# A decoder layer in float32: the dense products of 512 columns written as two of 256 columns

## The chip, the cores and the metric

The kernel runs on one core of a Trainium2 chip. The metric is the device time of one execution in microseconds. A core has a matrix engine (PE, TensorE), a vector engine (DVE, VectorE), a scalar engine (ACT, ScalarE), POOL (GpSimd) and SP (SyncE), which issues most DMAs. A product on PE has a stationary operand (the weights, loaded by an instruction of its own that the profile shows on a row PEld) and a moving operand, whose columns stream through; its result goes to PSUM, in banks of 512 float32 columns.

## The reference

One layer of a decoder over 512 tokens of width 1024: a norm, one combined projection, four token mixers (sliding-window attention, a convolution module, forgetting attention, block-sparse attention), each projected and gated, an output projection, and a feed-forward part with a causal convolution of width 3.

```python
h = rmsnorm(x, ln1_g)
z = h @ w_in
...
proj = jnp.einsum('bsnc,ncd->bsnd', branches, w_br)
merged = jnp.einsum('bsnd,bsnd->bsd', gates, proj)
x = x + merged @ w_out
h2 = rmsnorm(x, ln2_g)
u = causal_depthwise_conv(h2 @ w_up, ffn_conv_w, ffn_conv_b)
g_ff, v_ff = jnp.split(u, 2, axis=-1)
return x + (jax.nn.silu(g_ff) * v_ff) @ w_down
```

A last norm follows. All tensors are float32.

## The kernel before

Activations lie transposed, 128 channels by 512 tokens, so a tile of the result is 128 output channels by all 512 tokens, which is one PSUM bank. To keep precision with the one-pass type float32r, each operand is split into a high part (a rounded copy, by ACT, line 179) and a low part (the rest, by DVE, line 180), and a product is made of three: high by high, low by high, high by low. The names are whi and wlo for weights, hh and hl for the normed activations (both 8 tiles of 128 channels deep), and y with two planes for the outputs of the mixers, 4 tiles deep.

The work is a list of units, written out in order. A dense unit is made by `t_mm` (lines 232 to 247): it takes a PSUM tile `dps` of three that rotate, and for each of nk tiles k multiplies (wh, mh), (wl, mh), (wh, ml) into it, 3 x nk products of 512 columns with the weights as the stationary operand. It serves the combined projection except for the v columns, the gates, the up-projection (nk = 8, moving hh and hl) and the branch projections (nk = 4, moving y). Not made by it are the v units (line 294, 24 products of 256 columns, the first four of them 264), the attention products (lines 451, 452, 506, 565, 566, 624), the output projection (lines 967 and 1009) and the down-projection (line 1118). In line 506 a head multiplies v, as the stationary operand, with PTh and then with PTl, in widths of 512, 384, 256 and 128; line 624 does the same for the sliding window in widths of 256 and 128 with va as the stationary operand (odd heads keep both parts in one tile PT). In line 1118 the activations ah and al are stationary and the weights move; its last tile of 128 tokens uses two banks of 256 columns each (`wps`), and its last 8 of 22 weight tiles lie resident in wdh and wdl, which take the buffers of hh and hl (same tags).

The main loop (from line 1393 on) takes the units in turn: pieces of attention heads go on PE ahead of the unit's own products, then the previous unit's result is taken out of PSUM, then the splits of the next weights and the loads are issued. PE runs its instructions in the order written; semaphores tell it when weights are split and when a PSUM bank is free. `DVE P` of line 472 is the scaling of the softmax, `DVE sm` of line 584 a sum in the sliding window's softmax.

Of the kernel before, what the change touches and what calls it, by code (L numbers as in the profile page):

```python
# [53 lines left out]
def hybrid_layer_kernel(ctx: ExitStack, tc: tile.TileContext, x, ln1_g, w_in, b_gate, b_fgate, sinks,  # L54
# [3 lines left out]
    PE, ACT, DVE, SP = nc.tensor, nc.scalar, nc.vector, nc.sync  # L58
# [20 lines left out]
    def dense_ps():  # L79
        return PD.tile([128, 512], F32, name="dps", tag="dps", bufs=3)  # L80
# [66 lines left out]
    class Raw:  # L147


        def __init__(self, parts, nk, w):  # L150
            self.parts, self.nk, self.w = parts, nk, w
            self.idx, self.left = len(raws), 0
            raws.append(self)
# [70 lines left out]
        return [Half(raw, slice(k, k + 4), slice(0, n)) for k in (0, 4)]  # L224


    class Unit:
        def __init__(self, hs, mm, ev, adv=True):
            self.hs, self.mm, self.ev, self.adv = hs, mm, ev, adv
# [2 lines left out]
    def t_mm(hf, c0, mh, ml, nk):  # L232

        def go(mid=None, at_k=0):
            ps = dense_ps()
            h = hf[0]
            n = 0
            for k in range(nk):
                if mid and k == at_k:
                    mid()  # L240
                wh, wl = h.hi[:, k, c0:c0 + 128], h.lo[:, k, c0:c0 + 128]
                for a, b in ((wh, mh(k)), (wl, mh(k)), (wh, ml(k))):
                    PE.matmul(ps, lhsT=a, rhs=b, start=n == 0, stop=n == 3 * nk - 1)  # L243
                    n += 1
            return ps
        return go
# [959 lines left out]
    for half, end in ((0, NF), (1, KRES)):  # L1206
        for k0 in range(0, end, 4):
            nk = min(4, end - k0)
# [292 lines left out]
```

## Time and profile before

| | us |
|---|---|
| median of 3 runs (lowest to highest) | 1014.49 (1014.19 to 1014.76) |
| the profiled execution's own time | 1014.47 |
| its span, first to last instruction | 1012.7 |
| PE busy | 1001.2 |
| PEld busy (weight loads) | 824.6 |
| DVE busy | 667.0 |
| ACT busy | 448.3 |

Products on PE overlap in its pipeline: a product's duration in the profile is the time from its start to its modelled end, and the next one starts well before that. What a product takes from the time is the distance from its start to the next start. It is read from the timeline (start times) or from the chain of work that ended last, where a run of products of one kind stands as one piece with a start, a length and a count.

### The profile page before, as it was taken

How to read it: one execution, taken by the hardware profiler on the slowest of the kernel's cores; microseconds unless marked ns; L12 is line 12 of the kernel's file. 1: busy time of each engine (PE TensorE's matmuls, PEld its weight loads, DVE VectorE, ACT ScalarE, POOL GpSimd, SP SyncE). 2: the span in 40 equal slices, each digit the busy share in tenths (PEclk: the TensorE clock that was granted, in tenths of full speed). 3: DMA queues.
4: the chain of work that ended last, by engine and by line, in shares of the span. 5: the costliest groups of instructions: out<-in, count | busy, mean ns of one | idle time of the engine just before them, and what ended most of it. 6: DMA issues, size and time to landing. Idle time of an engine off the chain costs nothing.

```text
span 1012.7 us, 12462 instructions
## 1 busy us (share of the span) xinstructions
PE 1001.2 (99%) x4840; PEld 824.6 (81%) x4840; DVE 667.0 (66%) x1188; ACT 448.3 (44%) x782; POOL 23.2 (2%) x49
## 2 busy tenths in 40 slices
PE   8999999999999999999999999999999999999997
PEld 6878887989888888888888888888888888888886
DVE  6557777777878688896665445677776677733404
ACT  6435455455455545556423233443444444432202
POOL 1300000000000000000000000000000000000000
PEclk9999999999999999999999999999999999999999
DMA  7335522132233133232135430232223223334102
GB/s 254 102 113 185 164 85 85 42 105 81 66 108 121 42 83 100 64 99 93 42 125 205 149 125 1 84 125 84 83 94 114 83 84 99 130 124 146 63 1 84
DMA packets 101099, 102.18 MB, mean 101 GB/s; under 512 B 3377, under 2 KB 88544, under 8 KB 101040
## 3 DMA queue, kind: packets, MB, share of 16 engines
q1 hardware_dynamic: 99264, 99.31, 31.0%
q0 software_dynamic: 1200, 1.03, 0.4%
q10 hardware_dynamic: 576, 1.05, 0.3%
q8 instruction: 38, 0.62, 0.2%
q14 instruction: 21, 0.17, 0.1%
HBM read 99.10 MB, written 7.51 MB: 105 GB/s over the span
## 4 chain that ended last, share of the span: by engine, by line
PE 92%; DVE 4%; ACT 2%; issue 1%; DMA 1%; SPq 0%; DVEq 0%; ACTq 0%
PE dps L243 63%; PE wps L1118 8%; PE dps L1118 5%; PE dps L294 4%; PE dps L1009 2%; PE wps L967 2%; PE tps L479 2%; PE yps L506 1%; PE sps L452 1%; PE sps L451 1%; ACT P L434 1%; PE yps L624 1%; DMA raw<-in_w_in_dram 1%; DVE stE L383 1%; DVE P L472 1%
## 5 line engine op out<-in xcount | busy, mean ns | idle before, releaser
L243 PE MATMUL dps<-hh,whi 128*128 128x512 f32 x848 | 336.0, 396 | 0.0
L243 PE MATMUL dps<-hh,wlo 128*128 128x512 f32 x848 | 335.3, 395 | 0.0
L243 PE MATMUL dps<-hl,whi 128*128 128x512 f32 x848 | 335.1, 395 | 0.0
L180 DVE TENSOR_TENSOR wlo<-raw,whi 128x1024 fp32r<-128x1024 f32 (+1 forms) x152 | 185.5, 1222 | 95.4 <-ACT whi L179 95.2
L179 ACT ACTIVATE whi<-raw 128x1024 fp32r<-128x1024 f32 (+1 forms) x152 | 159.6, 1055 | 98.0 <-PE wps L1118 37.9
L243 PEld LDWEIGHTS dps<-hh,wlo 128*128 128x128 f32 x848 | 159.8, 188 | 37.1
L243 PEld LDWEIGHTS dps<-hl,whi 128*128 128x128 f32 x848 | 159.1, 188 | 37.1
L243 PEld LDWEIGHTS dps<-hh,whi 128*128 128x128 f32 x848 | 159.2, 188 | 36.8 <-ACT v L304 0.2
L434 ACT ACTIVATE P<-P,nm 128x128 f32<-128x128 f32 (+2 forms) x96 | 50.9, 531 | 76.4 <-DVE nm L432 75.8
L243 PE MATMUL dps<-y,whi 128*128 128x512 f32 x256 | 83.6, 397 | 0.0
L707 DVE SCALAR_TENSOR_TENSOR co<-hc,pcB,co 128x489 f32<-128x489 f32 (+25 forms) x120 | 82.5, 729 | 0.4
L1082 DVE SCALAR_TENSOR_TENSOR uy<-u,pcC,uy 128x511 f32<-128x511 f32 x88 | 65.8, 747 | 1.5
L243 PEld LDWEIGHTS dps<-y,whi 128*128 128x128 f32 x256 | 48.3, 189 | 10.9
L1074 DVE TENSOR_TENSOR u<-dps,rb 128x512 f32<-128x512 f32 x44 | 30.2, 687 | 37.3 <-PE dps L243 34.6
L243 PE MATMUL dps<-y,wlo 128*128 128x512 f32 x128 | 50.7, 396 | 0.0
L492 ACT ACTIVATE PTh<-tps 128x512 fp32r<-128x512 f32 (+1 forms) x48 | 24.4, 525 | 43.6 <-PE tps L479 43.3
L1118 PE MATMUL wps<-whi,al 128*128 128x512 f32 (+1 forms) x116 | 42.6, 367 | 0.0
L1118 PE MATMUL wps<-whi,ah 128*128 128x512 f32 (+1 forms) x116 | 42.6, 367 | 0.0
L1118 PE MATMUL wps<-wlo,ah 128*128 128x512 f32 (+1 forms) x116 | 42.5, 366 | 0.0
L1096 ACT ACTIVATE ah<-uy 128x512 fp32r<-128x512 f32 x22 | 13.9, 632 | 60.4 <-DVE uy L1095 60.4
L536 ACT ACTIVATE ytmp<-yps 64x512 f32<-64x512 f32 x24 | 14.3, 595 | 48.6 <-PE yps L506 25.0
L1088 ACT ACTIVATE uy<-uy 128x512 f32<-128x512 f32 x22 | 13.9, 632 | 43.7 <-DVE uy L1082 43.7
(250 smaller groups left out, 1291.9 us busy)
## 6 DMA issues: line engine op xcount, KB each, us to landing
raw<-in_w_up_dram SPq DMA_DIRECT2D x22, 1024.0 KB, 5.1
raw<-in_w_in_dram SPq DMA_DIRECT2D x40, 512.0 KB, 3.9
raw<-in_w_in_dram SPq DMA_DIRECT2D x14, 1024.0 KB, 5.1
raw<-in_w_down_dram SPq DMA_DIRECT2D x10, 1024.0 KB, 5.0
raw<-in_w_br_dram SPq DMA_DIRECT2D x16, 512.0 KB, 3.4
Gw<-Gd SPq DMA_DIRECT2D x8, 640.0 KB, 6.9
x<-in_x_dram SPq DMA_DIRECT2D x8, 512.0 KB, 8.4
raw<-in_w_out_dram SPq DMA_DIRECT2D x4, 1024.0 KB, 4.9
```

The source lines that it names most:

```text
L179: yield ACT.activation(self.hi, src, AF.Copy)
L180: yield DVE.tensor_tensor(self.lo, src, f(self.hi), op=OP.subtract)
L243: PE.matmul(ps, lhsT=a, rhs=b, start=n == 0, stop=n == 3 * nk - 1)
L294: PE.matmul(ps[:, :n], lhsT=l, rhs=r[:, k % 4, :], start=not done, stop=len(done) == 3 * KD - 1)
L434: ACT.activation(P[:, sl], P[:, sl], AF.Exp, bias=nm[:, i:i + 1], scale=-1.0, accum_out=sm[:, i:i + 1])
L479: PE.transpose(ps[:, c:c + 128], o["P"][:, PO[qb] + kb * 128:PO[qb] + kb * 128 + 128], ident)
L492: ACT.activation(o["PT"][0][:, sl], ps[:, :c], AF.Copy)
L707: DVE.scalar_tensor_tensor(co[c][:, d:], hc[:, :S - d], col_cw(CW - 1 - d, c), co[c][:, d:], op0=OP.mult, op1=OP.add)
L967: PE.matmul(oa[t], lhsT=l, rhs=r, start=k == 0 and i == 0, stop=k == KD - 1 and i == 2)
L1074: DVE.tensor_tensor(u, ps, n2["rb"], op=OP.mult)
L1082: DVE.scalar_tensor_tensor(y[:, d:], u[:, :S - d], col_fw(2 - d, j), y[:, d:], op0=OP.mult, op1=OP.add)
L1118: PE.matmul(ps, lhsT=l, rhs=r, start=k == first_k and i == 0, stop=k == last_k and i == 2)
```

## The change

In a dense unit the first product, which has the start flag and so begins a new sum in the bank, stays at 512 columns. Each later one becomes two of 256 columns, the first half of the moving operand into the first half of the bank and then the second half into the second, both with the same stationary tile. The stop flag of the last product goes to both of its halves.

```diff
+    def mm2(ps, l, r, start, stop):
+
+        for c, n in ((0, 512),) if start else ((0, 256), (256, 256)):
+            PE.matmul(ps[:, c:c + n], lhsT=l, rhs=r[:, c:c + n], start=start, stop=stop, skip_group_check=True)
+
...
                 for a, b in ((wh, mh(k)), (wl, mh(k)), (wh, ml(k))):
-                    PE.matmul(ps, lhsT=a, rhs=b, start=n == 0, stop=n == 3 * nk - 1)
+                    mm2(ps, a, b, n == 0, n == 3 * nk - 1)
                     n += 1
```

In PE's program the first dense units meet here: the end of one and the beginning of the next, whose first two products wait for the splits of its weights (in brackets, with the semaphores' numbers). Before:

```order
L243 MATMUL dps<-hh,whi 128x512
L243 MATMUL dps<-hh,wlo 128x512
L243 MATMUL dps<-hl,whi 128x512
L243 MATMUL dps<-hh,whi 128x512 [waits DVE_49,Activation_49]
L243 MATMUL dps<-hh,wlo 128x512 [waits DVE_49]
L243 MATMUL dps<-hl,whi 128x512
```

And now, where the line is that of the new helper:

```order
L230 MATMUL dps<-hh,whi 128x256 x2
L230 MATMUL dps<-hh,wlo 128x256 x2
L230 MATMUL dps<-hl,whi 128x256 x2
L230 MATMUL dps<-hh,whi 128x512 [waits DVE_49,Activation_49]
L230 MATMUL dps<-hh,wlo 128x256 [waits DVE_49]
L230 MATMUL dps<-hh,wlo 128x256
L230 MATMUL dps<-hl,whi 128x256 x2
```

Each product but the unit's first stands as two, the wait of a product stands at its first half, and nothing changes its place. The orders of DVE, ACT, POOL and SP are the same as before.

## Rows read from the trace of the kernel before

**Rows 1.** The page: busy time, granted clock, instruction queue, chain by engine and line.

```profile
PE 1001.2 (99%) x4840; PEld 824.6 (81%) x4840; DVE 667.0 (66%) x1188; ACT 448.3 (44%) x782; POOL 23.2 (2%) x49
...
PEclk9999999999999999999999999999999999999999
...
q8 instruction: 38, 0.62, 0.2%
...
PE 92%; DVE 4%; ACT 2%; issue 1%; DMA 1%; SPq 0%; DVEq 0%; ACTq 0%
PE dps L243 63%; PE wps L1118 8%; PE dps L1118 5%; PE dps L294 4%; PE dps L1009 2%; PE wps L967 2%; PE tps L479 2%; PE yps L506 1%; PE sps L452 1%; PE sps L451 1%; ACT P L434 1%; PE yps L624 1%; DMA raw<-in_w_in_dram 1%; DVE stE L383 1%; DVE P L472 1%
```

**Rows 2.** Waits of PE: us in total, times, longest.

```profile
PE tps L479 <- DVE P L472: 1.1, 1, 1.1
PE tps L753 <- DVE sm L584: 0.9, 1, 0.9
```

**Rows 3.** Groups by shape on PE, line 243: count, busy us, mean ns.

```profile
L243 PE MATMUL dps<-hh,whi 128*128 128x512 f32 x848 | 336.0, 396 | 0.0
...
L243 PE MATMUL dps<-y,whi 128*128 128x512 f32 x256 | 83.6, 397 | 0.0
L243 PE MATMUL dps<-y,wlo 128*128 128x512 f32 x128 | 50.7, 396 | 0.0
```

**Rows 4.** The chain in order of time: start us, length us, piece, count.

```profile
46.18 5.70 PE dps L294 x48
...
645.84 237.63 PE dps L243 x1020
...
946.85 0.71 PE wps L1118 x6
...
983.38 0.71 PE wps L1118 x6
984.09 16.80 PE dps L1118 x72
1000.89 5.47 PE wps L1118 x48
```

**Rows 5.** Groups by shape on PEld, lines 243 and 506.

```profile
L243 PEld LDWEIGHTS dps<-hh,wlo 128*128 128x128 f32 x848 | 159.8, 188 | 37.1
...
L506 PEld LDWEIGHTS yps<-PTh,v 128*128 128x128 f32 x64 | 12.1, 188 | 1.4
L506 PEld LDWEIGHTS yps<-PTl,v 128*128 128x128 f32 x64 | 12.0, 188 | 1.4
```

**Rows 6.** Timeline of PE in one head of line 506: start us, us.

```profile
110.91 0.39 PE L506 MATMUL yps<-PTl,v 128*128 128x512 f32 x1
111.14 0.34 PE L506 MATMUL yps<-PTh,v 128*128 128x384 f32 x1
...
111.49 0.28 PE L506 MATMUL yps<-PTh,v 128*128 128x256 f32 x1
...
111.73 0.22 PE L506 MATMUL yps<-PTh,v 128*128 128x128 f32 x1
```

**Rows 7.** Timeline of PE in the last unit, first and thirty-first start of a stretch.

```profile
1001.08 0.28 PE L1118 MATMUL wps<-wdh,ah 128*128 128x256 f32 x1
...
1004.48 0.28 PE L1118 MATMUL wps<-wdh,ah 128*128 128x256 f32 x1
```

**Rows 8.** Timeline of PE in line 624, two heads: first and seventh start of each.

```profile
457.99 0.28 PE L624 MATMUL yps<-PTh,va 128*128 128x256 f32 x1
...
458.70 0.22 PE L624 MATMUL yps<-PTh,va 128*128 128x128 f32 x1
...
513.61 0.28 PE L624 MATMUL yps<-PTh,va 128*128 128x256 f32 x1
...
514.29 0.22 PE L624 MATMUL yps<-PTh,va 128*128 128x128 f32 x1
```

**Rows 9.** Windows, the last unit: length, busy us by engine, clock, DMA share, GB/s.

```profile
1001.00:1006.00 5.00, 5.00 (x47) 5.00 (x46) 3.57 (x11) 2.26 (x6) 0.00 (x0) 1.00 0.23 86
```

## What the change was predicted to do

> **What bounds the kernel now.** I read the page first: over the span of 1012.7 us PE has 99% busy time, the granted clock is at its upper level (2.4 GHz) in all 40 slices, and the chain that ended last is PE for 92% of its length, 63% of it line 243 alone, the line of the products that are changed [rows 1]. The waits of PE come next: after the first 13 us it waits for another engine twice, 1.1 and 0.9 us [rows 2]. So the time is the number of products on PE times the distance from one start to the next, and the question is that distance alone. The groups by shape count the products: line 243 has three groups of 848 with the activations hh or hl (one of them stands there) and 256 + 128 with y, 2928 in all, each of 512 columns [rows 3].
>
> Their mean duration of 396 ns is not what one costs, since products overlap in the pipeline: 2928 x 396 ns would be 1159 us, more than the span. The cost is read from stretches of the chain where nothing but such products runs. In the up-projection 1020 products of line 243 take 237.63 us, **233.0 ns each** [rows 4].
>
> **The change, part by part.** Each unit's first product (the one with the start flag) stays whole. A unit over hh and hl has 24 products: 2544 / 24 = 106 units; one over y has 12: 384 / 12 = 32 units. So 138 products stay as they are, and 2928 - 138 = **2790** become two of 256 columns. PE's products go from 4840 to 7630, and each new one brings a weight load of its own unless the chip leaves it out; the program names no load apart from its product for these types.
>
> *Does the second half load again?* Line 506 already multiplies twice with the same v as stationary, first PTh, then PTl. The loads there are 64 for PTh and 64 for PTl, 188 ns each, as long as those of line 243 [rows 5]. So a repeated weight tile is loaded again. The timeline of one such head gives a first price: a 512-column product there takes 0.23 us from start to start (110.91 to 111.14), and two of 256 columns with the same v take 0.24 us (111.49 to 111.73) [rows 6]. To two digits the pair is equal or a little dearer; the exact surplus needs longer rows.
>
> *What does a product of 256 columns cost in a row of such?* There are two answers in the trace, and they lie on the two sides of half of 233.0, which is 116.5 ns:
> - In 48 products of line 294 (the v units, each with another weight tile): 5.70 us, 118.8 ns. Six products of line 1118 that stand between products of 512 columns: 0.71 us, 118.3 ns; the chain has 14 such groups of six, from 946.85 to 983.38 us, all at 0.71 [rows 4].
> - In the last unit of the down-projection, from 1001.08 to 1004.48 us, 30 products of line 1118 take 3.40 us, **113.3 ns** [rows 7]. Right ahead of it 72 products of 512 columns with the same tiles take 16.80 us, 233.3 ns each [rows 4].
> - Line 624 shows both with the same names on both sides: six products of 256 columns take 0.71 us at 457.99 us (118.3 ns) and 0.68 us at 513.61 us (113.3 ns) [rows 8].
>
> I take 118.3 ns: it holds in most places of the trace, in the only long row with units like the changed ones beside it (line 294) as in the short groups of line 1118, and whole and halved products stand mixed there, as they will in a changed unit. A pair is then 2 x 118.3 = 236.7 ns against 233.0: +3.7 ns, and 2790 x 3.7 = **+10.3 us**. The bounds: by line 294, 237.5 - 233.0 = 4.5 ns, +12.6 us; by the tail, 226.7 - 233.0 = -6.3 ns, -17.6 us.
>
> *What the longer products give back.* PE comes about 1% later to each wait, some 4 us in the middle of the kernel. The two waits there hold 1.1 + 0.9 = 2.0 us [rows 2]; the producers (softmax of line 472, layer norm) are held by PE only in part, so I take these two as covered: **-2.0 us**. The bounds are 0 and -2.0. The waits of the first 13 us lie ahead of all changed products and stay.
>
> *What costs nothing.* The wait that stood at a product of 512 columns stands at the first half, and the second half follows with no wait of its own; no semaphore is added, and the orders of VectorE, ScalarE and SP are the same. VectorE is busy for 66% and ScalarE for 44% of the span [rows 1], so nothing of theirs is late next if PE is slower; were PE faster by 1.7%, both would still have room, with the two waits above growing by at most some us. PE's instructions come by the queue q8, now 38 packets and 0.62 MB in 0.2% of the DMA time [rows 1]. Products and their loads go from 9680 to 15260, so some 60 packets, one in about 17 us; beside a queue that is idle for 99.8% this stays hidden. The 5.47 us of the last unit [rows 4] and what follows it are not touched.
>
> **Sum.** The profiled execution took 1014.47 us, 1.8 more than its span, and the median of the runs is 1014.49, so no correction is needed: 1014.47 + 10.3 - 2.0 = **1022.8 us**, slower by 0.8%.
>
> **Rivals.**
> *Faster: the 113-ns rhythm.* In the tail the products of 256 columns keep 113.3 ns for the whole unit [rows 7], though VectorE is busy for 3.57 and ScalarE for 2.26 of 5.00 us there [rows 9], so it isn't quiet that makes it. Moreover wdh and wdl take the buffers of hh and hl (tags "hh" and "hl"), and the tail reads their halves as the changed units will. If the changed units fall into this rhythm, a pair costs 226.7 ns: 2790 x -6.3 = -17.6 us, 996.9 us. It decides at 116.5 ns for one half; below that the change gains. Against it: the 48 products of line 294, at units like the changed ones, don't have it [rows 4], and line 624 has it at one head and not at another with tiles of the same names [rows 8], so the buffers alone don't decide. Chance 0.22, with the cases in between.
>
> *No change: the pair streams as one.* If the cost goes by columns alone, with none for an instruction, 256 columns cost 116.5 ns and a pair 233.0: 1014.5 us, or 1012.5 if the two waits go. The pair on line 506, 0.24 us beside 0.23, is only a rounding away from this [rows 6]. It would also be the result if the load of the second half were left out or cost nothing. Chance 0.15.
> The Trainium skill, "TensorE: Matmul & The Clock Gate", Part 2 (step 1, LDWEIGHTS), says that load and product are separate instructions so that one load can serve many products; by that rule the second load of each pair would be needless. The trace doesn't agree as far as these products go: 64 and 64 loads stand on line 506 [rows 5]. By the rule the time would be that of this rival.
>
> *Much slower: the load becomes the bound.* A load is recorded with 188 ns. If two loads of a pair followed each other at that length, a pair would take 376 ns, 143 more, and 2790 x 143 ns = +399 us. Line 294 has a load for each of its products and goes on at 118.8 ns, so the loads overlap. Something of it, at over 1028 us, gets 0.05.
>
> **How the numbers follow.** A difference of 0.2%, 2 us, is about what a measurement of this kernel can tell from no change. The forecast (1017 to 1028 us, from halves at 117.3 ns with both waits covered up to line 294's price with none) has 0.58; with the load-bound case, slower has 0.63. No change has 0.15, faster 0.22. Cases of both signs are in play, so the range reaches from the full tail rhythm, 996, to the upper end of the forecast, 1028; beyond it lie the load-bound case and what a price off these rows would give.
>
> **What would show it.** In the changed kernel's chain a dense unit alone on PE should take 0.233 + 23 x 0.237 = 5.68 us instead of 5.59; if it takes 5.45, the tail's rhythm holds. The weight loads of the dense line should number 5718; 2928 would mean that the second is left out. The waits of lines 472 and 584 on PE should be gone. The prediction is wrong if the halves stand closer than 116.5 ns; it is wrong in another way if gaps of PE by its own sequencer appear between them.

## The result, and the profile after

| | before | after |
|---|---|---|
| median, us (lowest to highest) | 1014.53 (1014.19 to 1014.76) | 1021.53 (1021.50 to 1022.05) |
| profiled execution, us | 1014.47 | 1021.50 |
| its span, us | 1012.7 | 1019.7 |
| products on PE | 4840 | 7630 |

The changed kernel is slower: ratio 1.007, interval [1.0058, 1.0082], or 7.0 us. The prediction was 1022.8 us.

The page of after answers to [rows 1]: busy time of each engine, the instruction queue, and the chain by engine.

```profile
PE 1008.5 (99%) x7630; PEld 959.6 (94%) x7630; DVE 667.4 (65%) x1188; ACT 448.4 (44%) x782; POOL 23.2 (2%) x49
...
q8 instruction: 60, 0.98, 0.4%
...
PE 92%; DVE 4%; ACT 2%; issue 1%; DMA 1%; SPq 0%; DVEq 0%; ACTq 0%
```

PE is still 92% of the chain and busy for 99% of the span. Its busy time grew by 7.3 us, about as much as the span (7.0). The instruction queue carries more but has work in 0.4% of the DMA time. So the time went into the products themselves. The lines moved down by five, and the dense products now stand on line 230, the helper.

The weight loads of that line by shape (count, busy us, mean ns), which answer to [rows 5]:

```profile
L230 PEld LDWEIGHTS dps<-hh,wlo 128*128 128x128 f32 x1696 | 267.0, 188 | 5.3
L230 PEld LDWEIGHTS dps<-hl,whi 128*128 128x128 f32 x1696 | 259.8, 188 | 0.0
L230 PEld LDWEIGHTS dps<-hh,whi 128*128 128x128 f32 x1590 | 246.7, 188 | 0.8 <-ACT v L309 0.2
L230 PEld LDWEIGHTS dps<-y,whi 128*128 128x128 f32 x480 | 67.1, 189 | 0.0
L230 PEld LDWEIGHTS dps<-y,wlo 128*128 128x128 f32 x256 | 41.6, 189 | 1.5
```

They sum to 5718, one for each product of the line (PE has 7630 products in all): the second half's load, with the same weights, is made again, and it is as long as any other.

The chain of after (start us, length us, piece, count), to be laid beside [rows 4]:

```profile
59.53 5.65 PE dps L230 x47
...
530.65 62.53 PE dps L230 x513
...
650.55 239.99 PE dps L230 x1998
...
991.14 16.80 PE dps L1123 x72
1007.95 5.47 PE wps L1123 x48
```

And two pieces of the chain of before that don't stand in [rows 4]:

```profile
59.31 5.59 PE dps L243 x24
...
527.04 61.53 PE dps L243 x264
```

The long piece is the up-projection. Its 1020 products became 1998, so 978 were doubled, and it grew from 237.63 to 239.99 us: **2.4 ns a pair**, so a pair takes 235.4 ns instead of 233.0. The piece from 530.65 us on, where the branch projections (moving y) lie among the gates, has 249 pairs (513 - 264) and grew by 1.00 us, 4.0 ns a pair. The tail, which the change doesn't touch, kept its 16.80 and 5.47 us to the digit.

The waits of PE in after, as in [rows 2]:

```profile
PE tps L484 <- DVE P L477: 1.0, 1, 1.0
PE tps L758 <- DVE sm L589: 0.6, 1, 0.6
```

They hold 1.6 us instead of 2.0. So the products cost about 7.4 us more, and the waits gave back 0.4.

### The profile page after: what moved, and what is told of

It reads as the page before. It is cut to its first block, busy times and chain, and to the rows that moved or that the text cites. A ratio compares the mean times of both kernels' runs of the same rounds, so it can differ in the third digit from the quotient of the medians.

```text
span 1019.7 us, 18052 instructions
## 1 busy us (share of the span) xinstructions
PE 1008.5 (99%) x7630; PEld 959.6 (94%) x7630; DVE 667.4 (65%) x1188; ACT 448.4 (44%) x782; POOL 23.2 (2%) x49
## 4 chain that ended last, share of the span: by engine, by line
PE 92%; DVE 4%; ACT 2%; issue 1%; DMA 1%; SPq 0%; DVEq 0%; ACTq 0%
PE dps L230 63%; PE wps L1123 8%; PE dps L1123 5%; PE dps L299 4%; PE dps L1014 2%; PE wps L972 2%; PE tps L484 2%; PE yps L511 1%; PE sps L457 1%; PE sps L456 1%; ACT P L439 1%; PE yps L629 1%; DMA raw<-in_w_in_dram 1%; DVE stE L388 1%; DVE P L477 1%
## 5 line engine op out<-in xcount | busy, mean ns | idle before, releaser
L230 PE MATMUL dps<-hh,whi 128*128 128x256 f32 (+1 forms) x1590 | 338.6, 289 | 0.0
L230 PE MATMUL dps<-hl,whi 128*128 128x256 f32 x1696 | 337.7, 280 | 0.0
L230 PE MATMUL dps<-hh,wlo 128*128 128x256 f32 x1696 | 337.6, 280 | 0.0
L230 PEld LDWEIGHTS dps<-hh,wlo 128*128 128x128 f32 x1696 | 267.0, 188 | 5.3
L230 PEld LDWEIGHTS dps<-hl,whi 128*128 128x128 f32 x1696 | 259.8, 188 | 0.0
L230 PEld LDWEIGHTS dps<-hh,whi 128*128 128x128 f32 x1590 | 246.7, 188 | 0.8 <-ACT v L309 0.2
L230 PE MATMUL dps<-y,whi 128*128 128x256 f32 (+1 forms) x480 | 84.8, 290 | 0.0
L230 PEld LDWEIGHTS dps<-y,whi 128*128 128x128 f32 x480 | 67.1, 189 | 0.0
L230 PE MATMUL dps<-y,wlo 128*128 128x256 f32 x256 | 51.3, 282 | 0.0
L230 PEld LDWEIGHTS dps<-y,wlo 128*128 128x128 f32 x256 | 41.6, 189 | 1.5
```

What stands on the lines that cost most here:

```text
L230: PE.matmul(ps[:, c:c + n], lhsT=l, rhs=r[:, c:c + n], start=start, stop=stop, skip_group_check=True)
```

## The experiments

Two questions were open. Why does a pair cost 2.4 ns more? The theories were a load that a half barely covers (A), a fixed cost of one more product whatever its width (B), and the place of the tiles (C). Later expectations call a sharper form of A theory L, and B theory S. And why didn't the halves fall into the 113-ns rhythm of the tail [rows 7]? All comparisons are with the kernel before, run beside each.

### Where the tiles lie

The weight tiles whi and wlo begin 32 bytes off a border of 64 bytes in the program's layout, while the tail's wdh and wdl begin on one. An unused tile of 32 bytes moves whi and wlo onto the border, in the changed kernel (e1) and in the kernel before (e2).

```diff
     bfg = P0.tile([128, 8], F32, name="bfg")
+    pad = P0.tile([128, 8], F32, name="pad")
```

> The changed kernel with one unused tile of 32 bytes ahead of the weight tiles, so that whi and wlo, which began 32 bytes past a 64-byte border in each partition, begin on one, as hh, hl, wdh, wdl, ah and al do. Theory A (the extra weight load of a pair makes the surplus) and theory B (one more product has a fixed cost) expect no difference: 1021.5 us, dense units alone on PE at 5.62 to 5.67 us. Theory C (the place of the tiles decides between halves at 118 and at 113.3 ns; in the last unit moving and stationary tiles both begin on a border) expects halves at 113.3 ns in the 106 units over hh and hl: 5.45 us a unit, some 1000 us in all.

> The kernel before with the same unused tile of 32 bytes, and nothing else. A and B expect 1014.5 us. C expects no difference for products of 512 columns either, since those of the last units have both tiles on a border and take 233.3 ns; only v units and attention, whose tiles move too, might gain: at most (118.8 - 113.3) ns for some 450 products, 2.5 us, so 1012 to 1014.5 us.

The changed kernel took 1025.24 us, 1.0105 [1.009, 1.012]; the kernel before took **1011.6 us, 0.997 [0.9958, 0.9982]**. The up-projection in the chain of e1:

```profile
652.22 242.52 PE dps L231 x1998
```

And in that of e2:

```profile
644.49 236.76 PE dps L244 x1020
```

The border theory falls: the halves didn't come to 113 ns, they became slower. What was not expected is the size of the effect on products that are otherwise the same: +3.7 us in the changed kernel and -3.0 us in the kernel before; of these, +2.5 and -0.9 us lie in the up-projection. At equal layout the change costs 13.6 us here (1025.24 - 1011.6), 4.9 ns a pair, instead of 7.0; in the up-projection alone (242.52 - 236.76) / 978 = 5.9 ns instead of 2.4. So the sign of the surplus held in both layouts, and its size did not.

An unused tile of 64 bytes keeps whi and wlo off the border, as in the kernel before, and asks whether any shift would have done:

```diff
     bfg = P0.tile([128, 8], F32, name="bfg")
+    pad = P0.tile([128, 16], F32, name="pad")
```

> The kernel before with an unused tile of 64 bytes ahead of the weight tiles, which stay 32 bytes past a 64-byte border and move against hh and hl. If the border decided the 3.0 us that the tile of 32 bytes gave, this gives none: 1014.6 us. If the distance between the tiles that stream and load together decides, the time moves again, by up to 3 us to either side.

It took 1015.22 us, 1.0007 [0.9998, 1.0017], no difference. That fits the border as the cause of the 3.0 us of e2, as the expectation put it; with one shift to either side it is not shown. But its chain has another rhythm in the last unit:

```profile
645.93 237.98 PE dps L244 x1020
...
1001.60 5.67 PE wps L1119 x48
```

The 48 products of the last unit took 5.67 us instead of 5.47 [rows 4], about 118 ns each instead of about 114, though in the program's layout none of the tiles that this unit reads had moved. So the two rhythms of [rows 7, 8] don't follow from the place of the tiles alone. What chooses between them stays open, also whether this kernel always has the slower one there: only one of its executions was profiled.

### The order of the halves

For each k the first halves of the three products go first and then the three second halves, so that no two products in a row share their weights, and no load is a repeat of the one ahead of it.

```diff
-                for a, b in ((wh, mh(k)), (wl, mh(k)), (wh, ml(k))):
-                    mm2(ps, a, b, n == 0, n == 3 * nk - 1)
-                    n += 1
+                ts = ((wh, mh(k)), (wl, mh(k)), (wh, ml(k)))
+                for c in (0, 256):
+                    for i, (a, b) in enumerate(ts):
...
+                        PE.matmul(ps[:, c:c + 256], lhsT=a, rhs=b[:, c:c + 256], start=False, stop=e,
+                                  skip_group_check=True)
```

> The changed kernel with the halves of a pair apart: for each k the three products of the first half, then the three of the second half. So as many products and loads as in the changed kernel, but no two products in a row have the same weights. If a repeated weight tile makes the load cheaper (theory A in a weak form), halves go up to line 294's 118.8 ns, where weights change each time: 2790 x (237.5 - 235.4) = +5.9 us, 1027 us. Theory B, a fixed cost for each product, expects 1021.5 us.

It took 1025.0 us, 1.0102 [1.0087, 1.0117], 3.5 us more than after. The 46 halves of a unit in its chain:

```profile
661.21 5.46 PE dps L255 x46
```

They take 118.7 ns each, the price that theory A in its weak form gave, against 117.7 in after. The whole run lies between the two expectations, 1021.5 and 1027 us: it is 1.2 ns a pair more, no more than the 32 bytes of e1 made. So equal weights in a row save at most that little. Whether the 1.2 ns belong to the weights or to the rhythm can't be told from this run.

### Other widths: is the load a floor under a product?

If a pair costs a fixed surplus, 384 + 128 columns cost the same as 256 + 256. If each product must last as long as a load, the narrow one costs more than its columns.

```diff
-        for c, n in ((0, 512),) if start else ((0, 256), (256, 256)):
+        for c, n in ((0, 512),) if start else ((0, 384), (384, 128)):
```

> The changed kernel with pairs of 384 and 128 columns in place of 256 and 256. Theory B expects the same 1021.5 us: one more product, the same columns. Theory A, with loads that follow each other no faster than one in about 0.11 us and a load that begins only when the product before has begun, expects the product after the one of 128 columns to come 113 ns behind it, as on line 506 (0.06 us after PTh and 0.11 us after PTl at 128 columns): a pair takes 177 + 113 = 290 ns, 2790 x 57 ns = +159 us, 1173 us. If loads can be made up over a pair, 1021.5 us by A too.

It took **1158.19 us, 1.1415 [1.1396, 1.1434]**. The timeline of PE in a unit alone on the engine (start us, us; x2 is a pair), with its piece of the chain first:

```profile
737.25 289.93 PE dps L230 x1998
...
801.03 0.45 PE L230 MATMUL dps<-hh,whi 128*128 128x384 f32 x2
801.31 0.45 PE L230 MATMUL dps<-hh,wlo 128*128 128x384 f32 x2
801.60 0.45 PE L230 MATMUL dps<-hl,whi 128*128 128x384 f32 x2
```

The pairs start 0.285 us apart, not 0.235. The piece gives (289.93 - 237.63) / 978 = 53.5 ns more for a pair, 286.5 ns. Two products of 384 columns on line 506 take 0.35 us in [rows 6] (111.14 to 111.49), 175 ns each, which leaves some 112 ns of the pair beside the stream of the wide product: about what theory A gave (a pair of 290 ns), and nearly twice the 60 ns or so that 128 columns stream. A fixed cost of one more product (B) can't be all.

The single starts show where in the pair the time goes. PE:

```profile
800.45 0.39 PE L230 MATMUL dps<-hh,wlo 128*128 128x384 f32 x1
...
800.67 0.22 PE L230 MATMUL dps<-hh,wlo 128*128 128x128 f32 x1
800.73 0.40 PE L230 MATMUL dps<-hl,whi 128*128 128x384 f32 x1
```

And the load for the last of these three:

```profile
800.68 0.19 PEld L230 LDWEIGHTS dps<-hl,whi 128*128 128x128 f32 x1
```

The narrow product is followed after 0.06 us, and the wide one only after 0.22 us, not 0.175. The load of the next weights begins with the narrow product, at 800.68, and not before it. So the profile notes the next wide product as started after 0.06 us; that it then stands until its weights are in is a reading that fits these starts and the sum. By it, from the start of a product to the moment when the next can stream there is at least one load, some 112 ns.

The same with a split that is less uneven:

```diff
-        for c, n in ((0, 512),) if start else ((0, 256), (256, 256)):
+        for c, n in ((0, 512),) if start else ((0, 320), (320, 192)):
```

> The changed kernel with pairs of 320 and 192 columns. Rule M (a product keeps PE for the longer of its stream and a load of 112 ns, and a load isn't made up by a wider neighbour): 320 columns stream in about 147 ns (between the 117.7 of 256 and the 176.6 of 384), 192 in about 89, so a pair takes 147 + 112 = 259 ns, 26 more than one product: 2790 x 26 = +73 us, 1087 us. If only very narrow products were dear, or two loads could share a pair's time, a pair stays at 235 to 237 ns: 1021 to 1025 us.

It took 1083.05 us, 1.0675 [1.0657, 1.0692]. The chain's piece and three pairs of the timeline:

```profile
688.94 263.13 PE dps L230 x1998
...
760.46 0.42 PE L230 MATMUL dps<-hl,whi 128*128 128x320 f32 x2
760.71 0.42 PE L230 MATMUL dps<-hh,whi 128*128 128x320 f32 x2
760.97 0.42 PE L230 MATMUL dps<-hh,wlo 128*128 128x320 f32 x2
```

The surplus is (263.13 - 237.63) / 978 = 26.1 ns, against the 26 ns that the rule "the longer of stream and load" gave. An estimate by columns for the wide part, 233.0 x 320 / 512 = 146 ns, leaves 113 ns for the rest of the pair: about the same as with 128 columns. And the wide neighbour makes up for none of it, in either run.

### Shorter loads

To see whether that floor is the load, the stationary tile is cut to 64 columns for all products but the first of a unit, with halves (e6), with whole products (e7) and with 384 + 128 (e10). These three kernels leave out half of the output channels of those products. Of e6:

```diff
-            PE.matmul(ps[:, c:c + n], lhsT=l, rhs=r[:, c:c + n], start=start, stop=stop, skip_group_check=True)
+            m = 128 if start else 64
+            PE.matmul(ps[:m, c:c + n], lhsT=l[:, :m], rhs=r[:, c:c + n], start=start, stop=stop, skip_group_check=True)
```

> The changed kernel with stationary tiles of 64 columns in place of 128 in all products of dense units but each unit's first: output channels 64 to 127 of these products are left out. A load is then half as long, the streams are the same. Theory L (loads beside the stream make the surplus of a pair; a product lasts as long as the longer of stream and load, and 256 columns lie just above the load's 112 ns) expects the surplus gone: a pair at 233.0 ns or less, 1014.5 us or less. Theory S (the surplus is the stream's own, a fixed cost per product) expects 1021.5 us.

> The same with whole products of 512 columns: stationary tiles of 64 columns in all products of dense units but each unit's first, output channels 64 to 127 of these products left out. Theory S expects 233.0 ns a product and 1014.5 us. If a load slows the stream that runs beside it (theory L in its strong form), products fall below 233 ns; the shortest row of 512 columns seen is 225.8 ns, which would be 2790 x -7.2 = -20 us, 994 us.

The loads of e6 and one group of e7 (count, busy us, mean ns), each with its piece of the chain. First e6:

```profile
L231 PEld LDWEIGHTS dps<-hh,wlo 128*64 128x64 f32 x1696 | 215.7, 134 | 10.7
...
649.58 240.46 PE dps L231 x1998
```

And e7, with whole products:

```profile
L231 PEld LDWEIGHTS dps<-hh,wlo 128*64 128x64 f32 x848 | 114.1, 135 | 74.1
...
644.54 235.97 PE dps L231 x1020
```

The loads fell from 188 to 134 ns, but the halves didn't gain: 1021.07 us, 1.0064 [1.0049, 1.0079]. The whole products took 1011.14 us, 0.9965 [0.9953, 0.9978]. So the surplus of halves isn't the length of their loads; it is there with short ones too: (1021.07 - 1011.14) / 2790 = 3.6 ns for one more product. That whole products gained 3.4 us with short loads may be the load or a shift like that of e2, which was about as large; the two weren't told apart.

The Trainium skill, "TensorE: Matmul & The Clock Gate", section "Back-to-back issue gap", gives an isolated product, at the upper clock, a fixed part of 2.5 ns besides its columns. The runs lie at it and above it: 2.5 ns a pair by 7.0 us, 3.6 by e7 and e6, 4.9 by e2 and e1. The formula as a whole doesn't hold for these products: it gives 216 ns for 512 columns, and the runs show 233.0.

```diff
-        for c, n in ((0, 512),) if start else ((0, 256), (256, 256)):
-            PE.matmul(ps[:, c:c + n], lhsT=l, rhs=r[:, c:c + n], start=start, stop=stop, skip_group_check=True)
+        for c, n in ((0, 512),) if start else ((0, 384), (384, 128)):
+            m = 128 if start else 64
+            PE.matmul(ps[:m, c:c + n], lhsT=l[:, :m], rhs=r[:, c:c + n], start=start, stop=stop, skip_group_check=True)
```

> Pairs of 384 and 128 columns as in the run that took 1158.2 us, but with stationary tiles of 64 columns in all products of dense units except each unit's first (output channels 64 to 127 of these are left out). Rule M with a load half as long, some 56 ns, expects the product of 128 columns to need only its stream of 60 ns: a pair 177 + 61 = 238 ns, +4.6 ns, 1027 us. If the narrow product is dear for another reason than its neighbour's load, the time stays near 1158 us.

It took **1020.86 us, 1.0062 [1.0047, 1.0077]**, where the same widths with full loads took 1158.19. Its chain's piece and timeline:

```profile
650.13 240.04 PE dps L231 x1998
...
760.35 0.39 PE L231 MATMUL dps<-hh,wlo 128*64 128x384 f32 x2
760.58 0.39 PE L231 MATMUL dps<-hl,whi 128*64 128x384 f32 x2
```

Of the second pair, the narrow product and what follows it:

```profile
760.75 0.22 PE L231 MATMUL dps<-hl,whi 128*64 128x128 f32 x1
760.81 0.34 PE L231 MATMUL dps<-hh,whi 128*64 128x384 f32 x1
```

The pair is back at 0.23 us, 2.5 ns over a whole product with a full load (240.04 against 237.63 for 978 pairs) and 4.2 ns over one with a short load (235.97, e7). The narrow product is still followed after 0.06 us, and the wide one now after 0.17 instead of 0.22 us (760.58 to 760.75). So what a narrow product adds beyond its columns is the load that begins with it, and with a load that is short enough a pair costs a small surplus, of the same size with 384 + 128 as with 256 + 256 columns. The edit halves the outputs of a product along with its load, which no run here tells apart; the starts speak for the load. What makes the small surplus itself wasn't found.

The Trainium skill, same page, section "LDWEIGHTS (loading the stationary operand)", gives a load columns / 1.2 in ns, 107 for 128 columns. The runs agree in the slope: 64 columns fewer make the recorded load 188 - 134 = 54 ns shorter. The floor of e4 and e9, 112 to 113 ns, is a few ns longer than the page's load.

### Where else: the up-projection alone, and the tail

The change in the up-projection alone, 44 units, 1012 pairs:

```diff
-        for c, n in ((0, 512),) if start else ((0, 256), (256, 256)):
+        for c, n in ((0, 512),) if start or whole else ((0, 256), (256, 256)):
...
-                    mm2(ps, a, b, n == 0, n == 3 * nk - 1)
+                    mm2(ps, a, b, n == 0, n == 3 * nk - 1, mh is not nh)
```

> The change in the up-projection alone: 44 of the 138 dense units, 1012 of 2790 pairs; the other dense units keep whole products. The changed kernel lost 2.4 us in that stage (240.0 us for the pieces that took 237.6), 2.4 ns a pair. If the surplus is a cost of each pair, the run takes 1014.5 + 2.4 = 1016.9 us. If the surplus came from elsewhere (waits, what follows a unit), the stage keeps 237.6 us.

It took 1017.15 us, 1.0024 [1.0015, 1.0034]. The piece of its chain:

```profile
646.09 239.99 PE dps L230 x1998
```

The piece is as long as in after, 239.99 us, though all that stands ahead of it is whole again. So the surplus adds up by pairs, and isn't a matter of a delay that comes from earlier in the kernel: 1012 of 2790 pairs are 36% and bring 2.4 of 7.0 us, 35%.

Last, the halves in the tail itself, in the kernel before: products of 512 columns of line 1118 with k from the resident part on become pairs. This takes in the 72 products ahead of the last unit (over wdh and wdl), and also 96 products at the end of the first output half (over whi and wlo), which the expectation didn't speak of.

```diff
+            if w < 512 or k < KRES:
...
+            for c in (0, 256):
+                PE.matmul(ps[:, c:c + 256], lhsT=l, rhs=r[:, c:c + 256], start=False, stop=k == last_k and i == 2,
+                          skip_group_check=True)
```

> The kernel before, with the 72 products of 512 columns of the last three units ahead of the tail (ah and al by the resident wdh and wdl) as two of 256 columns, same weights, as in the changed dense units; dense units stay whole. They take 16.80 us before, 233.3 ns each. If the rhythm of 113.3 ns belongs to these tiles, 144 halves take 16.3 us and the run 1014.0 us. If it belongs to the last unit alone and pairs cost what they cost in dense units, 235.4 ns, they take 16.95 us and the run 1014.7 us. One look; the chain's piece of these products is what counts.

It ran once and took 1014.35 us beside 1014.51, which is no difference. Its chain says more:

```profile
883.37 39.02 PE wps L1120 x168
922.39 22.76 PE wps L1124 x192
...
984.50 16.33 PE dps L1124 x144
```

The same stretch of the first output half in the chain of before:

```profile
883.47 61.30 PE wps L1118 x264
```

Over wdh and wdl the halves took 16.33 / 144 = 113.4 ns, and the 72 pairs are 0.47 us shorter than the 16.80 us of [rows 4]: here halving gains. Over whi and wlo they took 22.76 / 192 = 118.5 ns; the 96 pairs are 0.46 us longer than whole products (96 x 61.30 / 264 = 22.3). The same line with the same kind of stationary tile (ah, al) shows both signs in one run, at two places, and they cancel.

## Why the prediction came out as it did

**The bound** was right. PE sets the end before and after, and no wait, queue or other engine took its place.

**The counts** were right: 2790 pairs, 7630 products, 5718 loads. The rival in which the second load is left out had its test there and fell. The rule that it rested on (the Trainium skill, "TensorE: Matmul & The Clock Gate", Part 2, step 1) isn't what these products show: 5718 loads stand on line 230 for 2928 uses of a weight tile.

**The price of a half** had the right sign, and the size was off: the term "+3.7 ns" measured 2.4 ns in the up-projection and 4.0 ns in the stretch with y, over all about 7.4 us / 2790 = 2.7 ns. I had chosen the 118.3 ns of line 1118's short groups [rows 4]; a half in the up-projection takes 117.7. The choice of the row with whole and halved products mixed, against the tail's 113.3, was the one that decided the sign. But the chance of the faster rival was rightly not small: e5 shows its rhythm on 72 pairs, and e1, e2 and e8 show that a few bytes or nothing visible shift such prices by 1 to 4 ns a product. The row couldn't give the price more closely than that. (The upper end of the forecast, 1028 us, is 1 us above what line 294's price with no wait covered gives, 1014.47 + 12.6 = 1027.1.)

**The waits** were the other mis-sized term: -2.0 us predicted, -0.4 measured. The step was "held by PE only in part, so I take these two as covered", and the sign that went with it, both waits gone, didn't come. The chains of both kernels around the first of the two waits show where it fails. Before:

```profile
160.27 1.36 PE dps L243 x6
162.20 0.96 ACT whi L179
...
174.15 1.28 DVE P L472 x4
175.81 5.70 PE dps L294 x48
```

After:

```profile
161.21 1.36 PE dps L230 x11
163.15 0.96 ACT whi L179
...
175.15 1.28 DVE P L477 x4
176.81 5.70 PE dps L299 x48
```

The chain that ends in the wait starts from six (now eleven) products of PE, and these begin 0.94 us later after the change. The split of weights and the softmax behind them begin 0.95 us later and end 1.00 us later. PE being late makes the producer late as well; a wait shrinks only by what PE loses between the product that releases the chain and the wait itself, and that is about 0.1 us here (1.1 to 1.0). The second wait gave back 0.3 us in the same way. Its chain from the products that release it to the end of the wait, before:

```profile
428.68 0.87 PE yps L624 x8
...
451.93 0.63 PE tps L753 x4
```

After:

```profile
431.50 0.89 PE yps L629 x8
...
454.77 0.63 PE tps L758 x4
```

Both ends come 2.8 us later, so of all that PE had lost by then the wait could give back only what PE lost in these 23 us. The bounds 0 and -2.0 held the result; the end that I took was the wrong one.

The two errors have opposite signs: some 2.9 us too much for the pairs (10.3 against 7.4) and 1.6 us too much given back. That the sum came within 1.3 us owes something to this.

**The rivals.** "No change" would have needed a half at 116.5 ns; e6 shows that even with short loads one more product has a price. "The load becomes the bound" named a real mechanism, with the wrong edge: the recorded 188 ns isn't what a load takes from the stream, some 112 ns is. Halves of 256 columns, at 117 to 119 ns, lie just above that edge, so halving pays only the small surplus, 0.7%; 320 + 192 columns, one step further, cost about 7%, and 384 + 128 about 14%.

## What to carry to other kernels

Cutting a product in two with the same weights doesn't save the second load: each added product pays a small price (2 to 6 ns here, by layout), and each should stream at least as long as one load takes (some 112 ns for 128 stationary columns, reached at 256 moving columns here), since a wide neighbour doesn't make up for a narrow one. What a wait on another engine gives back is counted from the instruction that releases the producer: if that stands on the engine which is slowed, nearly nothing comes back. Before a difference of 0.3% is put down to an edit, see what the same edit does with tiles shifted by some bytes.

## What the runs showed of the hardware that was not expected

An unused tile of 32 bytes makes the kernel before faster, 1011.6 us, 0.997 [0.9958, 0.9982], the fastest of the kernels here that compute the whole layer; the same tile makes the changed kernel slower, 1025.24 us. One of 64 bytes does nothing to the time (1015.22 us).

Products of 256 columns have two rhythms, about 113.4 and 118 ns, and one and the same last unit showed the one in the kernel before (5.47 us) and the other in e8 (5.67 us) with its tiles at the same places. Line 1118 showed both within one run (e5). Which of them a row of products takes wasn't found. The 64-byte border of the weights doesn't decide it alone (e1), nor does the length of a load (e6), nor the place of the tiles (e8, by one execution).
